# Expert weights in 2 MB double slots, and a ring of two doubles for split weights

## The chip, the cores and the metric

The kernel runs on one core of a Trainium2 chip. The time is device microseconds of one launch of the whole program, median of several runs. The profile is one further execution of the same program, recorded by the hardware profiler.

## What is computed

Two transformer blocks, each of two layers, on 256 tokens of width 1024, in fp32. What matters here is the feed-forward of the first block's second layer, a mixture of eight experts of which each token takes two:

```python
def moe_swiglu(h, w_router, w_gate, w_up, w_down):
    logits = (h @ w_router).astype(jnp.float32)
    top_val, top_idx = lax.top_k(logits, TOP_K)          # 2 of 8
    top_w = jax.nn.softmax(top_val, axis=-1)
    gates = jnp.sum(jax.nn.one_hot(top_idx, N_EXPERTS) * top_w[..., None], axis=-2)
    out = jnp.zeros_like(h)
    for e in range(N_EXPERTS):
        y = swiglu(h, w_gate[e], w_up[e], w_down[e])     # silu(h@gate) * (h@up) @ down
        out = out + gates[..., e:e + 1] * y
    return out
```

Each expert has 3 x 1024 x 3584 weights, 44 MB, all eight together 352 MB: most of the 575 MB that the program reads. Before this layer come a gated linear attention, a dense feed-forward and a stick-breaking attention; after it a second block with a gated delta rule, two convolutional feed-forwards and a latent attention.

## The kernel before

**The experts (`experts`, L998).** The eight experts are taken in order of how many tokens they have, in four pairs of places (0,1) to (6,7); the even place of a pair has room for 96 tokens, the odd one for 64. An expert's weights are cut into 42 chunks of 1 MB, 128 partitions x 2048 columns: 28 for gate and up (three passes of 8 chunks, one of 4), 14 for down. `passes` (L265) gives the order: within a pair the two experts' passes alternate, then come the down chunks of the first and of the second expert. `gate_up` (L1045) and `down` (L1100) ask for one chunk at a time with `ahead.next` and run 24 (96 tokens) or 16 (64 tokens) recorded matmuls of 512 columns on it, or twice as many of 256.

**The loads ahead (`Ahead`, L214).** `fill` traces loads on SP's queue, in order, as long as a count of slots allows; `next` gives back the chunk asked for, counts the slot of the chunk before it as free and calls `fill` again. `home` (L256) says where chunk i of the 336 goes: of the first 39 chunks, 8 of every 13 go alternately into tiles tagged `raw` and `hl`, and 5 into general 512-column units (each of these 1 MB chunks by four DMAs of 256 KB with rows of 2 KB, L242); from chunk 39 on all alternate between `raw` and `hl` (one DMA of 1 MB with rows of 8 KB, L237). `raw` and `hl` have four buffers each (`RAWB, HLB = 4, 4`), so that a load waits for the matmuls of the chunk eight places earlier. The first `ahead.fill()` stands in `moe` (L868, the call at L941), before the gather of the first expert's tokens.

**The two tags in the rest of the kernel (`weights`, L367).** All other matrices come by `raw` (L358): a DMA of up to 2048 columns into a `raw` tile (L363). `weights` then splits it into a high and a low part, at most 1024 columns at a time: each piece gets an `hl` tile of its own, 2 x 1024 columns, one ACT copy (L401) and one DVE subtraction (L402). A `weights` call of 2048 columns takes two such tiles; one of 1024 columns or fewer takes one. `lin_w` and `lin_x` run the matmuls (L344) on both tiles of a call, first one group of outputs with all the rows of both, then the next. In the first attention the projection L688 has only 16 output columns and is one call with one `hl` tile; all other calls before the experts take two. After the experts the first call is that of L1338, again with 16 columns.

**Buffers.** Tiles come from pools; the program that schedules the kernel gives a tile a buffer of its tag once one is free, and takes it back when the last instruction that touches the tile (anywhere in the program) is done. It orders the instructions of an engine by their place in the program, but lets later ones pass while an earlier one has no buffer. General units (`unit`, 52 buffers) hold everything else: activations, the residual stream `x`, the gathered tokens `xg`.

**Around the branch.** After the first gate/up pass of the second pair `general` (L947) puts a branch on PE, ACT, DVE and POOL for the rare case that an expert has more tokens than room; it is not taken.

Of the kernel before, what the change touches and what calls it, by code (L numbers as in the profile page):

```python
# [8 lines left out]
F32 = mybir.dt.float32  # L9
F32R = mybir.dt.float32r  # L10
# [9 lines left out]
P = 128  # L20
# [7 lines left out]
NE = 8  # L28
CH = 2048
SUB = 1024  # L30
RAWB, HLB = 4, 4
EXTRA, FIRST = 5, 39
GS = 32
WORKERS = [mybir.EngineType.PE, mybir.EngineType.Activation, mybir.EngineType.DVE, mybir.EngineType.Pool]
CAPS = (96, 64, 96, 64, 96, 64, 96, 64)
# [105 lines left out]
class Weights:  # L141


    def __init__(self):
        self.at, self.items, self.size = {}, [], 0
# [33 lines left out]
    def expert(self, inp, e):  # L179

        gate, up = (inp[n][0, e].reshape(KD, P, EDIM) for n in ("moe_w_gate", "moe_w_up"))
        parts = []
        for a, w, kc in steps():
            for k0 in range(0, KD, kc):
                parts.append(np.stack([m[k0:k0 + kc, :, o:o + w] for m in (gate, up) for o in (a, a + w)], axis=1)
                             .transpose(2, 0, 1, 3).reshape(P, CH))
        down = inp["moe_w_down"][0, e].reshape(-1, 2, P, D)
        parts += [m.transpose(1, 0, 2).reshape(P, CH) for m in down]
        return np.stack(parts)


def steps():

    out, a = [], 0
    while a < EDIM:
        w = min(512, (EDIM - a) // 2)
        out.append((a, w, CH // (4 * w)))
        a += 2 * w
    return out
# [14 lines left out]
class Ahead:  # L214
# [3 lines left out]

    def __init__(self, K, queue, off, order, home, depth):
        self.K, self.queue, self.off, self.loaded, self.used = K, queue, off, [], 0  # L220
        self.order, self.home, self.depth, self.held = order, home, depth, [0, 0]

    def fill(self):
        K = self.K
        while len(self.loaded) < len(self.order):
            i = len(self.loaded)
            tag = self.home(i)
            kind = 0 if tag else 1
            if self.held[kind] == self.depth[kind]:
                break  # L230
            self.held[kind] += 1
            p, c = self.order[i]
            o = self.off[p] + c * P * CH
            src = K.a["wts"][bass.ds(o, P * CH)].rearrange("(p n) -> p n", p=P)
            if tag:
                t = K.wp.tile([P, CH], F32, name=K.nm("raw"), tag=tag, bufs=RAWB)
                self.queue.dma_start(t, src)  # L237
                blocks = [t[:, j * 512:(j + 1) * 512] for j in range(CH // 512)]
            else:
                blocks = [K.unit(name="raw") for _ in range(CH // 512)]  # L240
                for j, u in enumerate(blocks):
                    self.queue.dma_start(u, src[:, j * 512:(j + 1) * 512])  # L242
            self.loaded.append(blocks)

    def next(self, key):
        i = self.used
        assert self.order[i] == key, (i, self.order[i], key)
        self.used += 1
        if i:
            self.held[0 if self.home(i - 1) else 1] -= 1  # L250
        self.fill()
        out, self.loaded[i] = self.loaded[i], None
        return out


def home(i):  # L256

    c, r = divmod(i, 8 + EXTRA)
    if i >= FIRST:
        c, r = FIRST // (8 + EXTRA), i - FIRST  # L260
        return ("raw", "hl")[r % 2]
    return ("raw", "hl")[r % 2] if r < 8 else None


def passes(pairs):  # L265

    out = []
    for i, pair in enumerate(pairs):
        n = len(steps())
        if len(pair) == 1:  # L270
            out += [(pair[0], s) for s in range(n)]
        else:
            lag = 1 if i == 0 else 0
            a, b = pair
            for s in range(n + lag):
                out += [(a, s)] * (s < n) + [(b, s - lag)] * (s >= lag)
        out += [(p, None) for p in pair]
    return out


def loads(todo):

    first, at = [], 0
    for a, w, kc in steps():
        first.append(range(at, at + KD // kc))
        at += KD // kc
    return [(p, c) for p, s in todo for c in (range(at, at + EDIM // P // 2) if s is None else first[s])]


class Kern:  # L290
    def __init__(self, ctx, tc, wts, a, units=52):
        self.ctx, self.tc, self.nc, self.a, self.wts = ctx, tc, tc.nc, a, wts
        nc = self.nc
        self.cp = ctx.enter_context(tc.tile_pool(name="cp", bufs=1))
        self.wp = ctx.enter_context(tc.tile_pool(name="wp", bufs=2))
        self.tp = ctx.enter_context(tc.tile_pool(name="tp", bufs=6))
        self.up = ctx.enter_context(tc.tile_pool(name="up", bufs=units))
        self.dp = ctx.enter_context(tc.tile_pool(name="dp", bufs=1, space=DRAM))
        self.pm = ctx.enter_context(tc.tile_pool(name="pm", bufs=4, space=PSUM))
        self.px = ctx.enter_context(tc.tile_pool(name="px", bufs=4, space=PSUM))  # L300
        self.n = self.nts = 0
        self.rstd = self.cp.tile([P, 8], F32, name="rstd")
        self.hp = 150
        self.bg = None
        cst = self.cp.tile([P, CONSTS.shape[1]], F32, name="cst")
        par = self.cp.tile([P, PAR_COLS], F32, name="par")
        self.cst, self.par = cst, par
        self.c = {k: cst[:, o:o + w] for k, (o, w) in COFF.items()}
        self.pc, o = {}, 0
        for name, n in COLS + [("wr", KD * NE), ("dtb", 8), ("alog", 8)]:  # L310
            self.pc[name] = par[:, o:o + n]
            o += n
        self.ident = self.c["ident"]
        self.ones = self.cp.tile([P, P], F32, name="ones")
        nc.vector.memset(self.ones, 1.0)
# [51 lines left out]
    def weights(self, name, lead, k0, kc, cols, background=True):  # L367
        c = sum(b - a for a, b in cols)
        wh, wl = [], []
        raws = self.raw(name, lead, k0, kc, cols)  # L370
        while raws:
            part, w = [], 0
            while raws and w + raws[0].shape[1] <= SUB:
                part.append((raws[0], w))
                w += raws.pop(0).shape[1]
            hl = self.wp.tile([P, 2 * SUB], F32R, name=self.nm("whl"), tag="hl", bufs=HLB)
            hi, lo = hl[:, :w], hl[:, SUB:SUB + w]
            for raw, o in part:
                h_, l_ = (t[:, o:o + raw.shape[1]] for t in (hi, lo))
                self.split(h_, l_, raw)  # L380
            wh += [hi[:, i:i + c] for i in range(0, w, c)]
            wl += [lo[:, i:i + c] for i in range(0, w, c)]
        if background and self.bg is not None:
            self.bg_step()
        return wh, wl
# [272 lines left out]
    def load(self, name):  # L658
        x = FMT(self, KD, T, F32, "x")
        for i, u in enumerate(x.u):  # L660
            self.nc.sync.dma_start(u.rearrange("p (k t) -> p k t", k=2), self.a[name][:, 2 * i:2 * i + 2, :])
        return x
# [205 lines left out]
    def moe(self, x):  # L868
        nc, pc, tc = self.nc, self.pc, self.tc
# [5 lines left out]
        first, stride = self.wts.experts()  # L875
# [56 lines left out]
        for t in range(2):  # L932
            self.mm(ps[:, :NE], self.ones, M[:, t, :], start=t == 0, stop=t == 1)
        nc.vector.tensor_copy(cnt, ps[:, :NE])
        pairs = [(p, p + 1) for p in range(0, NE, 2)]
        load = lambda r, engine: first + nc.values_load(
            place[0:1, r:r + 1], engines=[engine], min_val=0, max_val=(NE - 1) * stride,
            skip_runtime_bounds_check_because="one of eight experts' begins")
        ahead = Ahead(self, nc.sync, [first] * NE, loads(passes(pairs)), home, (8, EXTRA))
        self.warm(26)  # L940
        ahead.fill()  # L941
        early = self.gather((0,), CAPS, [0] * NE, hth, htl, rt)
# [4 lines left out]
        def general(live):  # L947
            n = nc.values_load(place[0:1, NE:NE + 1], min_val=-2 * P, max_val=2 * P, engines=WORKERS,
                               skip_runtime_bounds_check_because="a count of 256 tokens less a capacity")
            live = live + self.cx.u  # L950

            def touch():
                nc.vector.tensor_copy(srt, srt)
                for u in live:
                    nc.vector.tensor_copy(u[:, :1], u[:, :1])

            touch()
            with tc.If(n > 0, preferred_fallthrough_block=False):
                begins = [first] + [load(r, mybir.EngineType.Pool) for r in RANKS[1:]]
                for over in range(2):  # L960
                    one = [(p,) for p in range(NE)]
                    self.experts(x, hth, htl, srt, one,
                                 Ahead(self, nc.gpsimd, begins, loads(passes(one)), lambda i: None, (0, 1)), over)
                touch()

        self.experts(x, hth, htl, srt, pairs, ahead, early=early, general=general)
# [985 lines left out]
```

## Time and profile before

| | us |
|---|---|
| median of 3 runs | 2450.22 (2448.76 to 2451.84) |
| the profiled execution | 2445.43 |
| its span | 2443.8 |
| first expert matmul starts | 519.96 |
| last expert matmuls end (1358.80 + 1.93) | 1360.73 |
| stretch 520 to 1360: DMA engines' busy share, rate | 1.00, 408 GB/s |

Times in rows are microseconds from the start of the span unless marked ns. PE is the matmul engine, PEld its weight load, SPq the queue of the SyncE engine that issues DMAs. A row of a timeline gives start, length, engine, line, operation, output<-input and xcount; in brackets the idle time before it and what ended it. The end of a matmul is modelled. A wait is put down to what came last.

### The profile page before, as it was taken

The page shows a single profiled execution, that of the slowest core. Times are in us where ns is not written, and L with a number is a line of the kernel's source. Part 1 is how long each engine was busy: PE and PEld are TensorE (multiplying, and loading weights), DVE is VectorE, ACT ScalarE, POOL GpSimd, SP SyncE. Part 2 cuts the span into 40 slices and gives each one's busy share as a digit, 9 for nine tenths or more (in the row PEclk, how much of TensorE's full clock was granted, in tenths as well). Part 3 has the DMA queues.
Part 4 walks back from the last instruction along what each step waited for, and adds up shares of the span by engine and source line. Part 5 has one row for each costly group of instructions (what it writes and reads, how often), then busy time and mean ns, then how long its engine had stood idle before and what let it go on. Part 6 is the DMA issues. An engine that isn't in the chain of part 4 may idle for free.

```text
span 2443.8 us, 47068 instructions
## 1 busy us (share of the span) xinstructions
PE 2339.8 (96%) x20147; PEld 1688.9 (69%) x20147; DVE 1127.8 (46%) x2307; ACT 818.6 (33%) x1385; POOL 56.5 (2%) x81
## 2 busy tenths in 40 slices
PE   8999999999998999999999999999999999898998
PEld 7788989763452353245235788787888888778998
DVE  4576645731011110001011548867754564786874
ACT  5544434621110110101111444422442342565653
POOL 0000000000000000000013000000000000010000
PEclk9999999999999999999999999999999999999999
DMA  7477677599999999999999511202223312232552
GB/s 280 170 273 280 255 298 298 186 346 381 398 417 409 419 415 416 418 418 412 419 418 412 193 53 69 65 23 87 97 71 117 104 65 100 82 104 87 189 182 95
DMA packets 91240, 581.74 MB, mean 238 GB/s; under 512 B 10279, under 2 KB 10535, under 8 KB 25744
## 3 DMA queue, kind: packets, MB, share of 16 engines
q1 hardware_dynamic: 89280, 572.43, 60.2%
q0 software_dynamic: 1744, 6.24, 0.7%
q8 instruction: 159, 2.61, 0.4%
q14 instruction: 57, 0.47, 0.1%
HBM read 575.48 MB, written 3.15 MB: 237 GB/s over the span
## 4 chain that ended last, share of the span: by engine, by line
PE 55%; DMA 9%; DVE 3%; ACT 2%; issue 1%; POOL 0%; DVEq 0%; ACTq 0%; POOLq 0%
PE mm L344 33%; DMA raw<-in_wts 9%; PE mm L1058 6%; PE ax L344 5%; PE mm L1111 5%; PE ax L1058 2%; PE ax L1111 1%; DVE whl L402 0%; ACT whl L401 0%; DVE Y L1128 0%; PE ax L1874 0%; PE ax L1085 0%; DVE sm L507 0%; PE ax L1701 0%; DVE sm L512 0%
## 5 line engine op out<-in xcount | busy, mean ns | idle before, releaser
L344 PE MATMUL mm<-h,whl 128*128 128x256 f32 (+2 forms) x3280 | 715.0, 314 | 10.4 <-DVE f L703 4.1
L344 PEld LDWEIGHTS mm<-h,whl 128*128 128x128 f32 (+1 forms) x3280 | 535.0, 189 | 63.1 <-ACT whl L401 12.7
L344 PE MATMUL mm<-l,whl 128*128 128x256 f32 (+2 forms) x1640 | 508.0, 312 | 0.0
L402 DVE TENSOR_TENSOR whl<-raw,whl 128x1024 fp32r<-128x1024 f32 (+3 forms) x330 | 386.7, 1178 | 252.6 <-ACT whl L401 252.3
L1058 PE MATMUL mm<-raw,xg 128*32 128x512 f32 (+1 forms) x4096 | 428.1, 543 | 27.9 <-DMA raw<-in_wts 21.3
L401 ACT ACTIVATE whl<-raw 128x1024 fp32r<-128x1024 f32 (+3 forms) x330 | 335.6, 1023 | 313.8 <-PE mm L344 281.9
L344 PEld LDWEIGHTS mm<-l,whl 128*128 128x128 f32 (+1 forms) x1640 | 308.0, 188 | 19.9 <-issue 0.3
L1058 PEld LDWEIGHTS mm<-raw,xg 128*32 128x32 f32 x4096 | 127.5, 110 | 279.2 <-issue 191.9
L1075 DVE TENSOR_TENSOR ht<-mm,t 64x512 f32<-64x512 f32 (+1 forms) x64 | 39.8, 622 | 460.0 <-ACT t L1074 458.4
L344 PE MATMUL mm<-fh,whl 128*128 128x256 f32 (+1 forms) x1056 | 235.9, 318 | 0.0
L1111 PE MATMUL mm<-raw,hT 128*32 128x256 f32 x3584 | 222.8, 381 | 4.9 <-DMA raw<-in_wts 4.7
L344 PEld LDWEIGHTS mm<-fh,whl 128*128 128x128 f32 x1056 | 174.0, 188 | 18.5 <-ACT whl L401 1.7
L1074 ACT ACTIVATE t<-mm 64x512 f32<-64x512 f32 (+1 forms) x64 | 34.4, 537 | 451.3 <-PE mm L1058 429.0
L1111 PEld LDWEIGHTS mm<-raw,hT 128*32 128x32 f32 x3584 | 114.8, 110 | 83.8 <-DMA raw<-in_wts 5.4
L344 PE MATMUL mm<-fl,whl 128*128 128x256 f32 (+1 forms) x528 | 166.5, 315 | 0.0
L1058 PE MATMUL ax<-raw,xg 128*32 128x512 f32 (+1 forms) x1024 | 125.7, 539 | 0.0
L1128 DVE COPY Y<-mm 32x256 f32<-32x256 f32 x32 | 13.4, 418 | 220.9 <-PE mm L1111 214.5
L344 PEld LDWEIGHTS mm<-fl,whl 128*128 128x128 f32 x528 | 99.1, 188 | 7.4
L344 PE MATMUL mm<-f,whl 128*128 128x256 f32 (+1 forms) x732 | 97.9, 290 | 2.1 <-ACT f L401 2.1
L344 PEld LDWEIGHTS mm<-f,whl 128*128 128x128 f32 x732 | 91.1, 188 | 5.6 <-ACT f L401 2.9
L1126 ACT ACTIVATE Y<-mm 32x256 f32<-32x256 f32 x32 | 12.0, 375 | 218.0 <-DVE Y L1128 217.4
L1267 DVE SCALAR_TENSOR_TENSOR t<-mm,par,t 128x510 f32<-128x510 f32 (+1 forms) x88 | 53.8, 613 | 66.5 <-ACT t L1264 66.5
(463 smaller groups left out, 2448.4 us busy)
## 6 DMA issues: line engine op xcount, KB each, us to landing
raw<-in_wts SPq DMA_DIRECT2D x509, 1024.0 KB, 11.2
raw<-in_wts SPq DMA_DIRECT2D x64, 256.0 KB, 6.0
raw<-in_wts SPq DMA_DIRECT2D x8, 768.0 KB, 4.3
raw<-in_wts SPq DMA_DIRECT2D x12, 512.0 KB, 3.5
raw<-in_wts SPq DMA_DIRECT2D x8, 384.0 KB, 3.0
raw<-in_wts SPq DMA_DIRECT2D x4, 576.0 KB, 3.9
spill<-x POOLq DMA_DIRECT2D x8, 256.0 KB, 6.0
x<-spill POOLq DMA_DIRECT2D x8, 256.0 KB, 4.1
```

What stands on the lines that cost most here:

```text
L344: self.nc.tensor.matmul(out, lhsT, rhs, start=start, stop=stop)
L401: self.nc.scalar.activation(hi, src, AF.Copy)
L402: self.nc.vector.tensor_sub(lo, src, hi.bitcast(F32))
L1058: self.nc.tensor.matmul(pss[g][r * GS:(r + 1) * GS, :w], xg(k, g), blocks[o // 512][:, o % 512:o % 512 + w], start=k == 0, stop=k == KD - ...
L1074: nc.scalar.activation(sg[up], pss[g][gate, :w], AF.Silu)
L1075: nc.vector.tensor_mul(ht[up], pss[g][up, :w], sg[up])
L1111: self.nc.tensor.matmul(y[g][q * GS:(q + 1) * GS], hT[k][g], blocks[o // 512][:, o % 512:o % 512 + 256], start=k == 0 and g != 1, stop=k = ...
L1126: self.nc.scalar.activation(dst, src, AF.Copy)
L1128: self.nc.vector.tensor_copy(dst, src)
L1267: nc.vector.scalar_tensor_tensor(o3[:, :, 1:], p3[:, :, :T - 1], w(0), o3[:, :, 1:], op0=ALU.mult, op1=ALU.add)
```

## The change

The host packs an expert's chunks in groups of four (by the chunk's number c within its expert): chunks 0 and 1 of a group are laid side by side, so that a partition's row has 16 KB; chunks 2 and 3 stay as they were. `home` now goes by c: `hl` for chunk 0 of a group (one DMA of 2 MB for chunks 0 and 1), `hl2` for chunk 1 (no DMA, the second half of the same tile), `raw` for chunks 2 and 3. The chunks in general units are now whole groups of four, three such groups among the first 36. The tag `hl` has two buffers of twice the width, and `weights` takes one tile for two pieces in turn: the first half when no half is left over, else the second half of the last tile.

```diff
-EXTRA, FIRST = 5, 39
+FIRST = 36
...
-        return np.stack(parts)
+        out = []
+        for c in range(0, len(parts), 4):
+            out += [np.concatenate(parts[c:c + 2], axis=1).ravel()] + [m.ravel() for m in parts[c + 2:c + 4]]
+        return np.concatenate(out)
...
     def fill(self):
...
             tag = self.home(i)
-            kind = 0 if tag else 1
-            if self.held[kind] == self.depth[kind]:
-                break
-            self.held[kind] += 1
+            if tag != "hl2":
+                n = 2 if tag == "hl" else 1
+                if self.held[tag] + n > self.depth[tag]:
+                    break
+                self.held[tag] += n
             p, c = self.order[i]
-            o = self.off[p] + c * P * CH
-            src = K.a["wts"][bass.ds(o, P * CH)].rearrange("(p n) -> p n", p=P)
-            if tag:
-                t = K.wp.tile([P, CH], F32, name=K.nm("raw"), tag=tag, bufs=RAWB)
+            o, n, part = (c, 1, 0) if c % 4 > 1 else (c - c % 4, 2, c % 4)
+            src = K.a["wts"][bass.ds(self.off[p] + o * P * CH, n * P * CH)].rearrange("(p n) -> p n", p=P)
+            cut = lambda t, a: [t[:, a + j * 512:a + (j + 1) * 512] for j in range(CH // 512)]
+            if tag == "hl2":
+                blocks = self.second
+            elif tag:
+                w, bufs = (2 * CH, HLB // 2) if tag == "hl" else (CH, RAWB)
+                t = K.wp.tile([P, w], F32, name=K.nm("raw"), tag=tag, bufs=bufs)
                 self.queue.dma_start(t, src)
-                blocks = [t[:, j * 512:(j + 1) * 512] for j in range(CH // 512)]
+                blocks, self.second = cut(t, 0), cut(t, CH) if tag == "hl" else None
             else:
                 blocks = [K.unit(name="raw") for _ in range(CH // 512)]
-                for j, u in enumerate(blocks):
-                    self.queue.dma_start(u, src[:, j * 512:(j + 1) * 512])
+                for u, part in zip(blocks, cut(src, part * CH)):
+                    self.queue.dma_start(u, part)
...
         if i:
-            self.held[0 if self.home(i - 1) else 1] -= 1
+            tag = self.home(i - 1)
+            if tag == "hl2":
+                self.held["hl"] -= 2
+            elif tag != "hl":
+                self.held[tag] -= 1
...
-def home(i):
+def home(i, c):
-    c, r = divmod(i, 8 + EXTRA)
-    if i >= FIRST:
-        c, r = FIRST // (8 + EXTRA), i - FIRST
-        return ("raw", "hl")[r % 2]
-    return ("raw", "hl")[r % 2] if r < 8 else None
+    if i < FIRST and i // 4 % 3 == 2:
+        return None
+    return ("hl", "hl2", "raw", "raw")[c % 4]
...
-        self.bg = None
+        self.bg = self.half = None
...
-            hl = self.wp.tile([P, 2 * SUB], F32R, name=self.nm("whl"), tag="hl", bufs=HLB)
+            if self.half is None:
+                self.half = self.wp.tile([P, 4 * SUB], F32R, name=self.nm("whl"), tag="hl", bufs=HLB // 2)
+                hl = self.half[:, :2 * SUB]
+            else:
+                hl, self.half = self.half[:, 2 * SUB:], None
...
-        ahead = Ahead(self, nc.sync, [first] * NE, loads(passes(pairs)), home, (8, EXTRA))
+        ahead = Ahead(self, nc.sync, [first] * NE, loads(passes(pairs)), home, {"hl": 4, "raw": 4, None: 4})
```

## Rows read from the trace of the kernel before

**Rows 1.** The page: span, busy tenths and DMA in 40 slices.
```profile
span 2443.8 us, 47068 instructions
...
PE   8999999999998999999999999999999999898998
...
DMA  7477677599999999999999511202223312232552
GB/s 280 170 273 280 255 298 298 186 346 381 398 417 409 419 415 416 418 418 412 419 418 412 193 53 69 65 23 87 97 71 117 104 65 100 82 104 87 189 182 95
```

**Rows 2.** Windows: stretch; length, busy of PE, PEld, DVE, ACT, POOL, PEclk, DMA share, GB/s.
```profile
550.00:575.00 25.00, 25.00 (x236) 7.91 (x232) 2.50 (x4) 2.37 (x4) 0.00 (x0) 1.00 0.97 360
875.00:900.00 25.00, 25.00 (x434) 14.27 (x437) 0.00 (x0) 0.00 (x0) 0.00 (x0) 1.00 1.01 418
975.00:1000.00 25.00, 24.35 (x228) 8.00 (x228) 3.75 (x6) 3.42 (x6) 0.00 (x0) 1.00 1.02 419
```

**Rows 3.** DMA issues: in 975 to 1000 us, then in 200 to 225 us.
```profile
raw<-in_wts SPq DMA_DIRECT2D x10, 1024.0 KB, 16.1
...
raw<-in_wts SPq DMA_DIRECT2D x6, 1024.0 KB, 4.9
```

**Rows 4.** SP's own waits, 480 to 1370 us: total, times, longest.
```profile
SPq L237 <- PE ax L1058: 223.4, 98, 8.6
SPq L237 <- PE mm L1058: 178.4, 103, 9.8
...
SPq L237 <- PE mm L344: 6.7, 4, 3.7
```

**Rows 5.** Groups on ACT by shape: before the experts (0 to 505 us), then after (1340 on).
```profile
L401 ACT ACTIVATE whl<-raw 128x1024 fp32r<-128x1024 f32 x128 | 134.3, 1058 | 113.9 <-PE mm L344 104.8 <-DMA raw<-in_wts 5.4 <-issue 2.0
L401 ACT ACTIVATE whl<-raw 128x512 fp32r<-128x512 f32 x4 | 2.5, 634 | 1.5 <-PE mm L344 1.5
L401 ACT ACTIVATE whl<-raw 128x128 fp32r<-128x128 f32 x1 | 0.3, 296 | 0.0
...
L401 ACT ACTIVATE whl<-raw 128x128 fp32r<-128x128 f32 x1 | 0.3, 310 | 20.4 <-DMA raw<-in_wts 20.4
```

**Rows 6.** Timeline of ACT: last split before, first split after the experts.
```profile
489.35 1.06 ACT L401 ACTIVATE whl<-raw 128x1024 fp32r<-128x1024 f32 x1 [0.31 <-PE mm L344]
...
1359.02 0.31 ACT L401 ACTIVATE whl<-raw 128x128 fp32r<-128x128 f32 x1 [20.40 <-DMA raw<-in_wts]
```

**Rows 7.** The residual stream's tiles: loaded at the start, still written at 911 us.
```profile
x<-in_x SPq DMA_DIRECT2D x4, 256.0 KB, 4.8
...
911.44 2.49 DVE L1158 TENSOR_TENSOR x<-ax,x 128x512 f32<-128x512 f32 x4 [0.30 <-PE ax L344]
```

**Rows 8.** Timeline of SP, 486 to 594 us: load issues by line.
```profile
486.32 14.18 SPq L237 DMA_DIRECT2D raw<-in_wts  x6
500.59 17.02 SPq L242 DMA_DIRECT2D raw<-in_wts  x20
522.80 18.36 SPq L237 DMA_DIRECT2D raw<-in_wts  x8
```

**Rows 9.** Timeline of PE: first two chunks, eight chunks of a 64-token place.
```profile
519.96 1.92 PE L1058 MATMUL mm<-raw,xg 128*32 128x512 f32 x16
521.70 1.04 PE L1058 MATMUL ax<-raw,xg 128*32 128x512 f32 x8
522.56 1.90 PE L1058 MATMUL mm<-raw,xg 128*32 128x512 f32 x16
...
565.17 0.66 PE L1085 MATMUL ax<-cst,ht 128*128 128x128 f32 x4
565.75 0.46 PE L1087 MATMUL ax<-cst,ht 64*128 64x64 f32 x4
566.14 13.94 PE L1058 MATMUL mm<-raw,xg 128*32 128x512 f32 x128
```

**Rows 10.** Timeline of PE at the branch, and windows around it.
```profile
751.31 3.64 PE L1058 MATMUL mm<-raw,xg 128*32 128x512 f32 x16 [6.49 <-issue]
...
744.00:752.00 8.00, 1.51 (x6) 0.23 (x8) 0.49 (x3) 1.77 (x3) 2.14 (x4) 0.80 1.01 411
752.00:760.00 8.00, 8.00 (x60) 2.56 (x56) 2.07 (x3) 0.00 (x0) 0.00 (x0) 0.77 0.96 375
```

**Rows 11.** Timeline of ACT and DVE in the dense feed-forward, around 256 us.
```profile
256.51 1.06 ACT L401 ACTIVATE whl<-raw 128x1024 fp32r<-128x1024 f32 x1 [0.59 <-PE mm L344]
257.93 1.06 ACT L401 ACTIVATE whl<-raw 128x1024 fp32r<-128x1024 f32 x1 [0.36 <-PE mm L344]
...
257.60 1.23 DVE L402 TENSOR_TENSOR whl<-raw,whl 128x1024 fp32r<-128x1024 f32 x1 [1.71 <-ACT whl L401]
```

**Rows 12.** DMA packets in 575 to 600 us, then in 875 to 900 us.
```profile
DMA packets 3477, 9.62 MB, mean 385 GB/s; under 512 B 385, under 2 KB 385, under 8 KB 2945
...
DMA packets 1432, 10.45 MB, mean 418 GB/s; under 512 B 159, under 2 KB 159, under 8 KB 159
```

**Rows 13.** Timeline of PE: the last chunk of the experts.
```profile
1358.80 1.93 PE L1111 MATMUL mm<-raw,hT 128*32 128x256 f32 x32 [0.61 <-DMA raw<-in_wts]
```

More of the change, by code (lines that the diff above doesn't have):

```diff
@@ L220, in __init__ @@
         self.K, self.queue, self.off, self.loaded, self.used = K, queue, off, [], 0
-        self.order, self.home, self.depth, self.held = order, home, depth, [0, 0]
+        self.order, self.home, self.depth = order, lambda i: home(i, order[i][1]), depth
+        self.held = dict.fromkeys(depth, 0)
     def fill(self):
@@ L962, in general @@
                     self.experts(x, hth, htl, srt, one,
-                                 Ahead(self, nc.gpsimd, begins, loads(passes(one)), lambda i: None, (0, 1)), over)
+                                 Ahead(self, nc.gpsimd, begins, loads(passes(one)), lambda i, c: None, {None: 1}), over)
                 touch()
```

## The prediction

> **What bounds the kernel now.** Begin with the page's slices [rows 1]: PE is busy nearly everywhere, but in the slices from about 650 to 1340 us the DMA engines are full as well, at 409 to 419 GB/s. The windows say which of the two sets the pace [rows 2]. In 550 to 575 us it is still PE (busy 25.00 of 25). From 875 us on it is the DMA: 418 to 419 GB/s, that is 2.51 us for a chunk of 1 MB. The DMA issues agree [rows 3]: a 1 MB load lands 16.1 us after its issue, where one alone takes 4.9, so some six are queued. SP's waits name the releaser [rows 4]: 201 waits, 402 us in all, for PE at L1058, so a load starts when the matmuls of an earlier chunk end. PE needs less than the DMA: 24 matmuls per chunk in a place of 96 tokens, of which [rows 9] show 16 begin in 1.74 us and 24 in 2.60 (I use 2.57), and 13.94 / 8 = 1.74 us per chunk in a place of 64. The ring of eight slots keeps a DMA-bound stage fed; what counts is how many slots are left.
>
> **Who holds the ring when the experts begin.** Count the `hl` pieces that `weights` takes before the experts, by the splits on ACT [rows 5]: 128 + 4 + 1 = 133, odd, because the 16-column call L688 takes one. The last is split at 489.35 us, the next, piece 134, at 1359.02 [rows 6]. Today that is nothing: each piece has a buffer of its own. With the change pieces go in twos into double tiles, so piece 133 is the first half of a double whose second half is handed to piece 134, behind all the experts. A buffer goes back only when the last instruction that touches its tile is done; `x` shows that such tiles are kept, loaded at the start and written in place at 911 us [rows 7] though many more than 52 units are made in between. So one of the two doubles is shut from 489 to about the end of the experts, and the expert loads have **one double slot**. A double can then be issued only when both chunks of the double before it are used up, and SP, which issues in order, holds the singles and units behind it.
>
> **The sum of the expert stage.** An expert has 11 doubles (c = 0, 4, ... 40); 88, less 3 whose groups go to units, is 85. From the end of one double's matmuls to the start of the next one's, W: the issue follows the matmuls by 0.06 us (they end at 521.70 + 1.04 = 522.74 [rows 9]; SP issues at 522.80 [rows 8]). No 2 MB load is in the trace. Below, it cannot beat two chunks at the queue's pace, 5.0 us; above, two quiet 1 MB loads in turn, 9.8 [rows 3]. I take one quiet load plus the bytes of a second, 4.9 + 2.51 = 7.4, since with the ring this short the queue ahead of it is empty. With 0.1 for the wake-up of PE, W = 7.5. PE on a double takes 2.57 + 2.78 (a second chunk with its tail) = 5.35 at 96 places, 3.5 at 64, mean 4.4, and 0.4 for the transposes that fall there ([rows 9] show 0.66 + 0.46 in one set): 4.8.
> - 85 x 4.8 + 84 x 7.5 = 408 + 630 = 1038 us. Two singles between doubles take PE 5.1 or 3.5 us, less than W, and hide in it.
> - Three stretches with six chunks between doubles, because of the units, are PE's: 6 x 2.57 - 7.5 = 8, 6 x 1.74 - 7.5 = 3, and 2 x 2.57 + 4 x 1.74 - 7.5 = 5: 16 us.
> - The branch and three pair switches, where PE pauses for other engines: 6.49 us of idle at the branch [rows 10], taken for all four: 26 us.
> Together 1080; the experts end near 520 + 1080 = 1600 in place of 1360.73 [rows 13]: **+239 us**. With the load at 5.0 PE's own 5.1 us of singles would set the pace, 408 + 84 x 5.1 + 42 = 878, +38; with 9.8 it is 84 x 2.4 = 202 more, +440. I stay at 7.4 because both its parts are rows, and let the range have W from 6.7 to 8.6.
>
> A rule speaks to this price. The Trainium skill, DMA: Bandwidth & Descriptors, section Anatomy of one DMA, gives for a load from GpSimd about 2.0 us plus bytes at 436 GB/s: an estimate by that page is 6.8 us for 2 MB and a sum 84 x 0.6 = 50 us smaller, near 2660. By it 1 MB would take 4.4, where the row has 4.9, and these loads are SP's, so I keep the row.
>
> **The clock.** After the 6.49 us of idle at the branch a group of 16 that takes 1.92 us takes 3.64, and two windows show a granted clock of 0.80 and 0.77, part of the time at the lower level [rows 10]: 0.20 x 8 + 0.23 x 8 = 3.4 us of work lost. Now PE idles for all 7.5 us where a double follows a double (c = 40, then the next place's c = 0), 7 times: up to 24 us. The other some 75 waits leave it idle 7.5 - 5.1 = 2.4 or 7.5 - 3.5 = 4.0 us; nothing in the rows shows such gaps costing clock, and half of a branch's loss at each would be 130. I take 20; bounds 0 and 130.
>
> **The other edits.**
> - Rows of 16 KB. From packets [rows 12], 16 engines x 25 us: 1273 rows of 8 KB make 0.314 us each; in the other window 400 - 532 x 0.314 over 2560 rows of 2 KB make 0.091. Four of these less one of 8 KB is 0.05 us for three packets' fixed cost, 0.017 each. A double saves an engine 8 packets, 0.14 us: 85 x 0.14 = 12 us at most, nothing if 16 KB goes as two packets. In the chain a load's whole transfer counts: -6.
> - Splits before the experts. Calls of two pieces straddle two doubles from L688 on, so the first piece's half comes free later: a split must wait for a call's end instead of the end of one of its pieces. Copy and subtraction take 1.06 + 1.23 us, and calls follow at 257.93 - 256.51 = 1.4 us per piece [rows 11], so up to 0.5 us of each of 66 calls is uncovered: 0 to 30, and SP's few waits on L344 (6.7 us in 4 [rows 4]) speak for little. I take 5. A gain has no source here: no piece gets its buffer earlier. After the experts calls are aligned again and their matmuls are longer: 0.
> - Start: with one double only chunks 0 to 3 are loaded ahead, not 13; this is in the sum, which waits from the first double on. The first matmul at 519.96 waits for the gather, not for weights, and stays.
> - Issues: 85 doubles, 154 singles and 48 unit loads, 287 in place of 381. SP spends the stage waiting [rows 4]: 0. The packing is the host's: 0. The last double lands as a whole where the last chunk came 0.61 us late [rows 13]: within the sum.
>
> **Sum**: 239 + 20 + 5 - 6 = 258. The profiled execution has 2445.43, so 2703; the median of the runs lies 4.8 above it: 2708, said as **2710**. Its own range: W between 6.7 and 8.6 (-70, +90), the clock -20 to +110, the rest -10 to +25; not all at once: 2640 to 2810.
>
> **Rivals.**
> - A, both doubles serve (the held half does not bind, because its buffer is taken back or piece 134 is scheduled in another tile): then the change does what it says. A double waits for the chunk seven, not eight, places before; the load of chunks 12 and 13 goes out one chunk of PE later, near 525.3 rather than 522.8, in a PE-bound stretch with 5 us at stake; PE's pauses cost about 5 more, the last double 2, the rows give back 6: 2456 (2445 to 2462). For it: the issuing order is the scheduler's, which I read from the code. Against: 133 is odd, and tiles are kept until their last use [rows 7]. 0.07.
> - B, faster. With both doubles free, the queue of 16.1 us [rows 3] outlasts every pause of PE (6.49 us [rows 10]), so the coarser ring costs nothing and the DMA-bound 700 us run at the rate of longer rows: -12 + 2, 2440. It decides at the share of the DMA engines in the ring stage: if it stays 1.00 through PE's pauses, B; if it dips, A. 0.05. What it improves on is the 418 GB/s of [rows 2]. The Trainium skill, same page, section Measured, has the rate rise with the size of a load, 425 GB/s at 16 MB; an estimate by it is 1.7% of 700 us, 12 us; B's own price is from [rows 12].
> - D, worse: the clock falls after nearly every wait (the 130 above), and W grows as a double's packets share the engines with the singles issued right behind it: 2830 or more. For it: the lower clock at the branch. Against: gaps of 2 to 4 us are short beside 6.49. 0.06.
> - Something else: 0.02.
>
> **Chances.** The forecast has 0.80; all its range is slower. What a measurement of this kernel can tell from no change is about 0.2%, 4.9 us. B is faster (0.05); of A some 0.04 lies within 0.2% and 0.03 above; slower 0.80 + 0.03 + 0.06 + 0.02 = 0.91. The range goes from the forecast's lower end to D, 2640 to 2830; A and B, 0.12, and what lies above are left out.
>
> **What would show it.** In the profile after: 85 loads of 2 MB landing in 7 to 8 us; SP waiting at its load line for PE, for the experts' matmuls, before every double; PE waiting for DMA 2 to 4 us every four chunks, and 7 us at seven places; the DMA share down to 0.8 and some 330 GB/s from 650 us on; experts' end near 1600; later stages as long as before. Wrong it would be if two 2 MB loads are ever under way at once in the expert stage, or if the DMA share stays near 1.00: then A or B. A lower granted clock all through the stage would say D.

## The result and the profile after

The changed kernel takes **2838.82 us**, median of 6 runs (2830.53 to 2843.7), beside 2451.03 (2447.81 to 2454.77) for the kernel before in the same rounds: a ratio of 1.158, interval [1.156, 1.159]. The direction and the shut slot are as forecast; the time lies 129 us above the forecast and 9 us above the end of its range, because two costs of that slot were sized too low. Line numbers of the changed kernel: L1058 is now L1073, L1111 L1126, L237 L246, L242 L251, L344 L355, L401 L416.

First the page, beside [rows 1]:

```profile
span 2837.5 us, 46364 instructions
...
PE   9999999987767786777766777999989999999998
...
PEclk9999999998989987999889988999999999999999
DMA  7467775597677766777667767212022232222453
GB/s 277 183 257 277 279 298 182 206 374 293 256 273 293 306 268 249 303 308 297 234 258 315 298 234 280 75 45 76 14 104 75 97 119 71 93 97 86 154 185 108
```

The stage in which the DMA was full has become one in which nobody is: in most slices PE and the DMA are each busy between 60 and 80% of the time, for 1230 us. Then the windows, columns as in [rows 2], of the expert stage, of the kernel after:

```profile
650.00:1000.00 350.00, 251.81 (x2768) 109.52 (x2764) 28.19 (x65) 23.84 (x47) 2.15 (x4) 0.89 0.73 283
1000.00:1400.00 400.00, 296.47 (x3470) 142.04 (x3465) 36.52 (x78) 29.87 (x62) 0.00 (x0) 0.88 0.71 277
1400.00:1741.00 341.00, 241.22 (x2660) 102.55 (x2655) 28.36 (x71) 26.16 (x53) 31.12 (x36) 0.86 0.72 283
```

and of the kernel before:

```profile
650.00:1000.00 350.00, 333.02 (x4228) 148.33 (x4224) 44.07 (x100) 35.98 (x72) 2.14 (x4) 0.99 1.01 415
1000.00:1340.00 340.00, 320.03 (x4072) 139.99 (x4070) 44.43 (x103) 40.60 (x82) 30.74 (x36) 0.99 1.01 417
```

A third of the rate is gone, and the granted clock has fallen to 0.86 to 0.89. What PE waits for, as the view of its waits has it (in total, times, longest):

```profile
PE mm L1073 <- DMA raw<-in_wts: 169.5, 49, 8.4
PE mm L1126 <- DMA raw<-in_wts: 109.5, 27, 5.7
```

76 waits for a load, about one per double. The chain that makes them is read from three views of one stretch. PE's timeline (a line runs over small gaps between chunks):

```profile
1204.45 1.92 PE L1073 MATMUL mm<-raw,xg 128*32 128x512 f32 x16 [2.58 <-DMA raw<-in_wts]
...
1217.90 7.07 PE L1073 MATMUL mm<-raw,xg 128*32 128x512 f32 x64 [1.05 <-DMA raw<-in_wts]
1229.88 9.17 PE L1073 MATMUL mm<-raw,xg 128*32 128x512 f32 x64 [4.91 <-DMA raw<-in_wts]
```

SP's timeline, in two short windows:

```profile
1209.87 1.37 SPq L246 DMA_DIRECT2D raw<-in_wts  x3
...
1221.61 1.36 SPq L246 DMA_DIRECT2D raw<-in_wts  x3
```

and its DMA issues, 650 to 1700 us:

```profile
raw<-in_wts SPq DMA_DIRECT2D x73, 2048.0 KB, 8.2
raw<-in_wts SPq DMA_DIRECT2D x132, 1024.0 KB, 11.2
```

At 1204.45 PE begins a double of a 96-token place. Its second chunk's matmuls end at 1209.81; 0.06 us later SP issues three loads at once, the next double and the two singles behind it. PE does two more singles, to 1215, and the transposes, then waits: the double lands after 8 us and its matmuls start at 1217.90. In the 64-token place that follows the double is used up at 1221.54, the next is issued at 1221.61 and starts PE at 1229.88, after 4.91 us of idle. In the whole stage no 2 MB load is issued before the one ahead of it has landed: one slot. And the half that shuts the other is seen on ACT:

```profile
1743.03 0.31 ACT L416 ACTIVATE whl<-raw 128x128 fp32r<-128x128 f32 x1 [30.91 <-DMA raw<-in_wts]
```

This is piece 134, the answer to the second line of [rows 6]; up to it the tile of piece 133 stays taken.

The stage runs from 524.65 (before 519.96 [rows 9]) to 1755.7 (before 1360.73 [rows 13]): 4.7 us later at its start, 390.3 longer, and what follows is 1.3 shorter; together the 393.7 by which the spans differ.

### The profile page after: what moved, and what is told of

It is laid out like the page before. It is cut to its first block, busy times and chain, and to the rows that moved or that the text cites. A ratio compares the mean times of both kernels' runs of the same rounds, so it can differ in the third digit from the quotient of the medians.

```text
span 2837.5 us, 46364 instructions
## 1 busy us (share of the span) xinstructions
PE 2450.3 (86%) x20147; PEld 1738.5 (61%) x20147; DVE 1123.7 (40%) x2309; ACT 806.7 (28%) x1383; POOL 56.7 (2%) x81
## 4 chain that ended last, share of the span: by engine, by line
PE 48%; DMA 17%; DVE 3%; ACT 1%; issue 1%; DVEq 0%; ACTq 0%
PE mm L355 29%; DMA raw<-in_wts 17%; PE mm L1073 6%; PE ax L355 5%; PE mm L1126 4%; PE ax L1073 1%; PE ax L1126 1%; DVE whl L417 1%; PE ax L1889 0%; DVE sm L522 0%; DVE Y L1143 0%; ACT whl L416 0%; PE ax L1716 0%; DVE x L1290 0%; DVE sm L527 0%
## 5 line engine op out<-in xcount | busy, mean ns | idle before, releaser
L355 PE MATMUL mm<-h,whl 128*128 128x256 f32 (+2 forms) x3280 | 717.9, 314 | 12.3 <-ACT h L561 3.6
L1073 PE MATMUL mm<-raw,xg 128*32 128x512 f32 (+1 forms) x4096 | 466.0, 592 | 169.6 <-DMA raw<-in_wts 169.5
L355 PEld LDWEIGHTS mm<-h,whl 128*128 128x128 f32 (+1 forms) x3280 | 537.0, 189 | 66.5 <-ACT whl L416 10.1
L355 PE MATMUL mm<-l,whl 128*128 128x256 f32 (+2 forms) x1640 | 509.6, 312 | 0.0
L1073 PEld LDWEIGHTS mm<-raw,xg 128*32 128x32 f32 x4096 | 146.2, 118 | 445.7 <-issue 299.0
L416 ACT ACTIVATE whl<-raw 128x1024 fp32r<-128x1024 f32 (+3 forms) x330 | 326.2, 1019 | 306.9 <-PE mm L355 206.0
L1126 PE MATMUL mm<-raw,hT 128*32 128x256 f32 x3584 | 261.4, 434 | 111.4 <-DMA raw<-in_wts 111.4
L355 PEld LDWEIGHTS mm<-l,whl 128*128 128x128 f32 (+1 forms) x1640 | 308.8, 189 | 19.2 <-issue 0.3
L1126 PEld LDWEIGHTS mm<-raw,hT 128*32 128x32 f32 x3584 | 127.2, 125 | 221.6 <-DMA raw<-in_wts 93.3
L355 PE MATMUL mm<-fh,whl 128*128 128x256 f32 (+1 forms) x1056 | 236.4, 318 | 0.0
L355 PEld LDWEIGHTS mm<-fh,whl 128*128 128x128 f32 x1056 | 174.1, 188 | 18.9 <-ACT whl L416 2.5
L355 PE MATMUL mm<-fl,whl 128*128 128x256 f32 (+1 forms) x528 | 166.4, 315 | 0.0
L1073 PE MATMUL ax<-raw,xg 128*32 128x512 f32 (+1 forms) x1024 | 129.2, 573 | 0.0
L355 PEld LDWEIGHTS mm<-fl,whl 128*128 128x128 f32 x528 | 99.1, 188 | 7.4
L355 PE MATMUL mm<-f,whl 128*128 128x256 f32 (+1 forms) x732 | 98.4, 290 | 0.0
L355 PEld LDWEIGHTS mm<-f,whl 128*128 128x128 f32 x732 | 91.5, 188 | 4.2 <-ACT f L416 1.3
```

The lines of the kernel that those rows point to most:

```text
L355: self.nc.tensor.matmul(out, lhsT, rhs, start=start, stop=stop)
L416: self.nc.scalar.activation(hi, src, AF.Copy)
L1073: self.nc.tensor.matmul(pss[g][r * GS:(r + 1) * GS, :w], xg(k, g), blocks[o // 512][:, o % 512:o % 512 + w], start=k == 0, stop=k == KD - ...
L1126: self.nc.tensor.matmul(y[g][q * GS:(q + 1) * GS], hT[k][g], blocks[o // 512][:, o % 512:o % 512 + 256], start=k == 0 and g != 1, stop=k = ...
```

## The experiments

**The half is given up.** One line, ahead of the expert loads:

```diff
+        self.half = None
         ahead = Ahead(self, nc.sync, ...
```

> The changed kernel, but the half double left over from the stick-breaking attention's output projection is given up before the expert loads are traced, so its tile goes back after its last real use; layout, ring and loads are unchanged. Theory (the held half shuts one of two doubles): both doubles serve, two 2 MB loads are under way at once, the DMA share of 650 to 1340 us is back near 1.0 and the time is 2440 to 2462, rival A's range; the gain over the changed kernel is 375 to 400 us. Rival 1 (the 2 MB loads, their rows of 16 KB or the coarser ring are slow by themselves): it stays above 2650.

Measured 2465.37 us (2460.24 to 2468.09), ratio to the kernel before 1.0056 [1.0043, 1.0069]. Windows and DMA issues (the latter 650 to 1340 us) of this run:

```profile
650.00:1000.00 350.00, 326.84 (x4236) 151.15 (x4239) 42.08 (x97) 33.53 (x68) 2.15 (x4) 0.99 1.00 414
1000.00:1340.00 340.00, 322.99 (x4082) 145.39 (x4078) 38.33 (x84) 39.31 (x79) 25.99 (x30) 0.98 1.00 413
```

```profile
raw<-in_wts SPq DMA_DIRECT2D x71, 2048.0 KB, 12.5
raw<-in_wts SPq DMA_DIRECT2D x127, 1024.0 KB, 13.2
```

373 of the 388 us go with one line that moves no byte, changes no load and no buffer count. The DMA share is 1.00 again; a double now lands 12.5 us after its issue, later than the 8.2 of the changed kernel, and costs nothing, since it waits in a queue and not alone. Rival 1 falls. The time lies 3 us above the range that was given, rival A's. Of the 14 us over the kernel before, 5 come before the experts, and the expert stage takes 851 us (524.91 to 1375.95) in place of 841; what those 10 us are was not tried.

**No call straddles.** The half is given up at the end of every call:

```diff
+        self.half = None
         if background and self.bg is not None:
```

> The changed kernel, but a half left over is given up at the end of every weights call, so that a call of two pieces always has one double and nothing is held over the experts. Theory: the expert stage as with the half given up before the experts (end near 1365), and the stretch before the experts begins its first expert matmul near 520 again instead of 524.65, since no call straddles two doubles: 2438 to 2458, 2 to 6 us faster than the run that gives up the half only before the experts (more if straddling also costs after the experts, where the held half's second part is not used up). Rival 1: above 2650. Rival 2 (straddling costs nothing, the 4.7 us are something else): within 2 us of the run that gives up the half only before the experts.

Measured 2463.86 (2461.28 to 2476.87), 1.0060 [1.0041, 1.0079]: no different from the run above, as rival 2 had it, and 6 us above the range. The first expert matmul starts at 523.57, not near 520. None of the 4.7 us before the experts can be put on straddling: among the profiles of the changed kernel and its variants that start lies at 523.69 to 526.55 with it, and without it at 523.57 here and at 525.97 in the run below that has the same calls and two loads to a double. The times of the splits in this run's trace show where the delay comes in: they fall behind the kernel before by 3.3 us in the first 115 us and by some 4 later. What in those first layers loses it was not tried; that a call's two pieces now give their buffers back together is a guess.

**Two loads to a double, held half as it is.** The chunks are packed as in the kernel before; of the edit, the loads:

```diff
-                self.queue.dma_start(t, src)
+                self.queue.dma_start(t[:, :CH], src)
+                if tag == "hl":
+                    self.queue.dma_start(t[:, CH:], at(1))
```

> The changed kernel with the held half as it is, but the old packing of 1 MB chunks with rows of 8 KB and each double loaded by two 1 MB DMAs into its halves; one double serves, as before. Theory (one double, each cycle pays the landing of a whole 2 MB load, 8.2 us): PE can begin when the first half lands, about 5.1 us after the issue, where PE's singles take 5.1 or 3.5 us; a cycle is 5.35 + 0.6 + 5.2 = 11.2 us at 96 places and about 10 at 64 (the second half lands 2.5 us after the first) in place of 14.6: about 84 x 4 = 290 us faster than the changed kernel, 2500 to 2620. Rival 1 (rows of 16 KB are slow by themselves): back to 2440 to 2470, as the rows are the only thing that changes. A third reading, that only the number of slots counts: no change, 2820 to 2850.

Measured 2623.57 (2616.36 to 2631.86), 1.0713 [1.0694, 1.0731]: 215 us back, 4 us beyond the range. Its windows' row for the stage:

```profile
524.00:1533.00 1009.00, 854.07 (x10004) 350.83 (x10004) 103.47 (x232) 93.69 (x187) 33.46 (x40) 0.97 0.87 343
```

The slot is as shut as before, and it is the landing of the whole load that is paid: from the end of one double's matmuls to the start of the next the median falls from 8.36 to 5.91 us, as PE starts on the first half. I had 5.2 there. Rows of 16 KB alone (rival 1) and a mere count of slots (the third reading) both fall.

**Matmuls of ones in the waits.** Twice, with different counts; the first had the cost of one wrong.

```diff
         self.fill()
+        if i >= FIRST and self.home(i) == "hl":
+            p, c = self.order[i - 1]
+            self.K.warm(52 if c == 41 else 28 if p % 2 else 16)
```

> The changed kernel with matmuls of ones (16, 28 or 52 of 128 columns, 0.148 us each, in a scratch tile) ahead of each double's first matmul from chunk 36 on, sized to the idle time there: 2.4, 4.1 and 7.7 us. Theory (the lower clock after each wait lengthens the matmuls of the doubles, 5.78 us a double where the fastest is 5.3 at 96 places and 3.6 at 64): the granted clock of the expert stage goes from 0.88 to near 1.0, a double takes 4.6 to 5.0 us and the time falls by 50 to 90 us, to 2750 to 2790. Rival (the doubles are long because PE waits within them, the clock costs little): no gain, up to 20 us slower by fills that overrun the wait.

Measured 2920.14 (2915.36 to 2920.78), 1.1906 [1.1888, 1.1923]: 81 us slower than the changed kernel. The timeline of PE shows why:

```profile
1196.39 1.04 PE L1076 MATMUL ax<-raw,xg 128*32 128x512 f32 x8
1197.36 3.84 PE L358 MATMUL ax<-ones 128*128 128x128 f32 x32
1201.13 1.92 PE L1076 MATMUL mm<-raw,xg 128*32 128x512 f32 x16
```

16 fills leave 32 records and take 3.84 us, not 2.4: in the median a double's first matmul now starts 1.3 us after its load has landed, where in the changed kernel it is 0.04. Then with 10, 17 and 32:

> The changed kernel with fills before each double as in the run with fills, but 10, 17 or 32 matmuls of ones: the run before showed that one such matmul leaves two records and takes 0.24 us, not 0.148, so that its fills of 3.8, 6.5 and up to 12 us overran the waits (issue to first matmul 10.45 us in place of 8.81) while a double fell from 5.78 to 5.06 us. Now 2.4, 4.0 and 7.7 us, inside the waits. Theory (the lower clock after each wait is 0.7 us of a double): doubles of 5.0 to 5.2 us, issue to first matmul 8.6 to 9.2, and 2770 to 2805, 35 to 70 us faster than the changed kernel. Rival (what a fill gives the clock it takes in delay, nothing to be had): 2825 to 2870.

Measured 2811.29 (2808.88 to 2813.14), 1.1467 [1.1449, 1.1486]: 27 us faster than the changed kernel, 6 short of the range. Over 524 to 1741 us, the windows of the changed kernel, then of this run:

```profile
524.00:1741.00 1217.00, 901.36 (x9825) 391.38 (x9827) 103.13 (x230) 92.70 (x185) 33.27 (x40) 0.88 0.72 281
```

```profile
524.00:1741.00 1217.00, 1129.75 (x12532) 651.50 (x12532) 111.16 (x243) 102.25 (x201) 33.39 (x40) 0.97 0.74 288
```

The clock goes from 0.88 to 0.97, and the mean double from 5.78 to 4.99 us of PE: 85 x 0.79 = 67 us. Not all of it is had, because the pause between doubles grows from 8.81 to 9.25 (84 x 0.44 = 37 us): some fills were ordered in among the singles and elsewhere, and some still ran past the landing. The rival's "nothing to be had" falls too, for the double's length; as a cure fills are a poor one.

The lower clock cost more than these 67 us, for three doubles of this run were stretched to 7.5, 16.0 and 17.5 us by fills among their own matmuls. Its cost can be read from the changed kernel itself. First two doubles of 64-token places in windows of their own (the granted clock is the third number from the end), then the start of a double of 96 tokens:

```profile
1217.90:1221.54 3.64, 3.64 (x36) 1.41 (x40) 0.00 (x0) 0.00 (x0) 0.00 (x0) 1.00 0.99 416
1229.88:1235.62 5.74, 5.74 (x36) 1.48 (x40) 0.00 (x0) 0.00 (x0) 0.00 (x0) 0.63 0.62 258
```

```profile
596.82 3.64 PE L1073 MATMUL mm<-raw,xg 128*32 128x512 f32 x16 [3.18 <-DMA raw<-in_wts]
```

At the full clock a double takes 3.64 us with 64 tokens and 5.36 with 96 (1204.45 to 1209.81); 42 of the one and 43 of the other make 383 us, and the 85 took 491. Of the 108 us between, 105 are the clock's: in 57 of the doubles the lower of its two levels, half the full one, was granted for part of the time.

**A ring of the same 6 MB, in single slots.** In the kernel before, two of the four `hl` tiles are kept through the experts, and chunks go `raw`, `hl`, `raw` in turn.

```diff
+        kept = [self.wp.tile([P, CH], F32, name=self.nm("kept"), tag="hl", bufs=HLB) for _ in range(2)]
...
-        ahead = Ahead(self, nc.sync, [first] * NE, loads(passes(pairs)), home, (8, EXTRA))
+        ahead = Ahead(self, nc.sync, [first] * NE, loads(passes(pairs)), home, (6, EXTRA))
```

> The kernel before, with two of the four hl tiles kept by two small tiles that are written before the expert loads and written again after the experts; the expert chunks outside units go raw, hl, raw in turn, so six single slots of 1 MB serve, the same 6 MB as one double and four singles. Theory (what costs is that the one double can't be loaded while it is used; six singles in turn keep the DMA fed): the queue is two loads shorter, the stage stays DMA-bound, 2450 to 2480. Rival (6 MB in place of 8 MB are too few whatever their size): above 2600.

Measured 2480.34 (2477.69 to 2481.9), 1.0113 [1.0097, 1.0129]: the theory's upper end. The same shut 2 MB cost 29 us here and 388 there. From its windows:

```profile
650.00:1000.00 350.00, 322.89 (x4156) 143.93 (x4156) 42.10 (x98) 34.21 (x70) 2.15 (x4) 1.00 0.99 406
```

**The rows, with both doubles serving.** As the run in which no call straddles, but with two 1 MB loads of 8 KB rows to a double, so that rows and number of loads both change.

> The run in which a half left over is given up at the end of every weights call, with the old packing and each double loaded by two 1 MB DMAs with rows of 8 KB. Only the rows and the number of DMAs differ from that run (2463.9). Theory (in a full queue rows of 16 KB gain nothing, the windows show 410 to 416 GB/s against 413 to 418 before): within 5 us, 2457 to 2469. Rival 1 (rows of 16 KB save 0.017 us per packet, 12 us in all, as the prediction bounded it): 2470 to 2478. Rival 2 (a double landing as a whole is what the 13 us over the kernel before are): 2449 to 2456.

Measured 2460.71 (2455.01 to 2470.62), 1.0040 [1.0025, 1.0056], 3.2 us under its partner, with overlapping runs: rows of 16 KB gain nothing that can be seen. Its windows, then its partner's:

```profile
650.00:1000.00 350.00, 328.63 (x4224) 147.41 (x4220) 42.76 (x99) 33.72 (x69) 2.16 (x4) 0.99 1.00 412
1000.00:1340.00 340.00, 322.15 (x4070) 138.38 (x4066) 37.80 (x83) 38.82 (x77) 26.02 (x30) 0.99 1.01 415
```

```profile
650.00:1000.00 350.00, 324.38 (x4212) 151.33 (x4208) 42.07 (x97) 33.55 (x68) 2.15 (x4) 0.99 0.99 409
1000.00:1340.00 340.00, 321.26 (x4098) 145.07 (x4096) 38.33 (x85) 39.66 (x79) 25.97 (x30) 0.99 1.00 417
```

**The rows, with one double.** As the changed kernel, one 2 MB load, but two rows of 8 KB a partition:

```diff
+    self.queue.dma_start(t.rearrange("p (d n) -> p d n", d=2), at(2).rearrange("(d p n) -> p d n", d=2, p=P))
```

> The changed kernel with the held half as it is and one DMA of 2 MB for each double, but with the old packing, so that a double is fetched as two rows of 8 KB a partition in place of one of 16 KB. Theory (8.2 us to land where the prediction had 7.4, because after a pause of the DMA the first 16 KB packet on each engine takes 1.35 us in the trace and the later ones 0.62, where the first of 8 KB takes 0.67 and the later ones 0.31): landing falls by about 0.35 us, 84 x 0.35 = 30 us, 2800 to 2820. Rival 1 (the landing goes by the size of the load alone): no change, 2830 to 2850. Rival 2 (longer rows do save 0.017 us a packet): 10 us slower, 2845 to 2860.

Measured 2823.14 (2819.44 to 2828.91), 1.1523 [1.1506, 1.1541]: 16 us faster than the changed kernel, 3 us beyond the range; both rivals fall. Its DMA issues, 650 to 1700 us:

```profile
raw<-in_wts SPq DMA_DIRECT2D x74, 2048.0 KB, 7.7
```

The load lands 0.5 us sooner, where the theory had 0.35, and the median pause falls from 8.36 to 7.94; a double takes 5.86 us of PE in place of 5.78 (+7 us in all), and the mean pause falls by 0.26 only (84 x 0.26 = 22 us).

## Why the prediction was right and wrong

**What held.** The odd count of pieces [rows 5, 6], a tile's buffer kept to its last use [rows 7], one double slot, 85 double loads, the release and issue 0.07 us apart (0.06 in [rows 8, 9]), and nothing after the experts. The counts and the place of the loss were right. The 4.7 us before the experts agree with the 5 by luck: straddling, the cause I gave, can't be seen to cost any of them. Two readings were off without weight in the sum: of the 7 places where a double follows a double, four go on to the next place's c = 28 and three to c = 0; and before the experts SP issued one double, three singles and the unit loads of a whole group, not chunks 0 to 3 alone.

**What failed is the size of two terms of the sum.** The stage was forecast at 408 + 630 + 42 + 20 - 6 = 1094 us; it took 1231, 137 more.

| term | forecast | measured |
|---|---|---|
| PE on the 85 doubles, clock apart | 85 x 4.8 = 408 | 491 - 105 = 386 |
| between doubles, with units and pauses | 630 + 42 = 672 | 84 x 8.81 = 740 |
| lower clock | 20 | 105 |
| rows of 16 KB | -6 | inside the 740 |

The 22 us too many in the first row hid part of the miss: the 0.4 us per double for transposes was not there, as they run in the pauses (between 1215 and 1217.90 above).

The first failing step is **"one quiet load plus the bytes of a second, 4.9 + 2.51 = 7.4"**. The landing is 8.2 us, and W, from matmuls' end to matmuls' start, had a median of 8.36 where I took 7.5: 84 x 0.86 = 72 us. The run with short rows shows about half of the difference: 7.7 with rows of 8 KB. The records of single packets say how. After a pause of the DMA the first 16 KB packet on each engine takes 1.35 us in the mean and later ones 0.61; with rows of 8 KB (the run with short rows) it is 0.93 and 0.31. What counts is the last of the sixteen first packets: it is done 2.25 us after the first of them began, with short rows 1.44. With seven or fifteen packets more behind it an estimate is 6.5 against 6.1 us, 0.4 of the 0.5 by which the landings differ. The price of a first packet grows with the row, and the DMA had paused before 71 of the 84 doubles, since no load is queued ahead of them. The other half of the difference stays open. In a full queue, in the run with the half given up, two packets of 8 KB take 0.63 us and one of 16 KB 0.63 as well: the 0.017 us per packet that I solved from two windows [rows 12] was not there, and the term of -6 has the wrong sign. An estimate by the Trainium skill, DMA: Bandwidth & Descriptors, section Anatomy of one DMA, whose figure is for loads from GpSimd, is 6.8 us for the landing; the trace's 8.2 is further from that than from my 7.4, so keeping the row was the better of the two.

The second, and the larger, is **"I take 20; bounds 0 and 130"** for the clock: it was 105. The reading "gaps of 2 to 4 us are short beside 6.49" was wrong. At 596.82 above, after 3.18 us of idle, 16 matmuls take 3.64 us, as long as after the 6.49 at the branch [rows 10], where at 1204.45 they take 1.92; of the 32 doubles after pauses of 2 to 4 us, 17 ran partly at the lower level. And PE's pauses at 96 tokens were longer than forecast, 3.8 us in the mean in place of 2.4; at 64 tokens they were 3.8 for 4.0. That nothing in the rows showed such gaps costing clock was no evidence, as the rows had no such gaps. I had put the clock's price on 7 places; it belongs to 57 doubles.

Third, the range. Each of these two lay inside its own bounds (W up to 8.6, the clock up to +110), but I wrote "not all at once" and cut the sum at 2810. They did come together. That they share a cause, the wait for the landing, is likely but only in part shown: with two loads to a double W is 2.4 us shorter and the clock is 0.97, but with short rows W is 0.4 us shorter and the doubles are no faster (5.86 us). Bounds that may share a cause are to be added.

**The rivals.** A came out when it was given its condition: both doubles serving give 2465, a little over its 2445 to 2462, and slower than the kernel before. The sign that was to decide between A and B misled: the DMA share stayed at 1.00, which was to mean B, and the time was A's. B is out, as rows gain nothing. D, at 0.06, gave the nearest number, and half of its reason holds: the clock costs 105 of the 130 us that D put there. The other half of D, a double that shares the engines with singles behind it, is not seen: the eight doubles with c = 40 have no single behind them and take 7.84 to 9.07 us from issue to matmul, the others a median of 8.30.

No version tried beats the kernel before; the nearest are 0.4 to 0.6% slower.

## What to carry to other kernels

Count how often a shared tile is handed out before a stage begins: an odd count leaves a part in the hands of someone who comes after the stage, and a ring of two large slots is then a ring of one. Fewer, larger slots lose more per slot: the same 6 MB fed the DMA in six slots and starved it as one double and four singles. When a price is a landing after a pause, price the first packet and what the pause does to the waiting engine together, and let their bounds add.

## What was not expected of the hardware

A row of 16 KB travels no faster than two of 8 KB (0.63 us against 2 x 0.315 in the queue-fed runs), and after a pause it is slower: 1.35 us as the first packet, where a first and a second one of 8 KB take 0.93 + 0.31 = 1.24. Pauses of PE of 3.8 us in the mean, one to a double, were enough to bring the granted clock of the stage's windows to 0.86 to 0.89 and to cost 105 us.
